# Hybrid decoder block on one core: the per-layer embedding's first loads in fewer DMAs on two queues, p's splits ahead of the weights', and the last row tile's last columns in two parts

## The chip, the core and the metric

One core of one Trainium2 chip runs the whole block in one launch. The metric is the device time of one execution, in microseconds (us). Beside it stands one profiled execution, in which the hardware profiler recorded each instruction; its times are what the views of the profile show.

The engines are TensorE (PE; its weight loads are a row of their own, PEld), VectorE (DVE), ScalarE (ACT), GpSimd (POOL), and SyncE (SP), which here issues the DMAs.

## The reference, cut to what matters

```python
h = x                                                     # (1024, 1024) f32
h = h + 0.5 * rms_norm(swiglu(rms_norm(h, g[0]), ffn1_gu, ffn1_down), g[1])
h = h + rms_norm(token_mixer(rms_norm(h, g[2]), ...), g[3])
h = h + 0.5 * rms_norm(swiglu(rms_norm(h, g[4]), ffn2_gu, ffn2_down), g[5])
gate = jax.nn.sigmoid(rms_norm(h, g[6]) @ w_ple_gate)     # (1024x1024) @ (1024x1024)
h = h + rms_norm(gate * (p @ w_ple), g[7])                # p (1024x256), w_ple (256x1024)
```

`rms_norm(y, g)` is `y * rsqrt(mean(y*y) + 1e-6) * g` over a row of 1024. The two lines at the end are the per-layer embedding: `p @ w_ple` depends on no other layer, and the gate needs the trunk's result.

## The kernel before, in words

The 1024 rows are worked in two halves of 512, and each half in four row tiles of 128. Every f32 operand of a matrix product is split into a high and a low part (`split`, L138 to L140): the high part is a cast to fp32r on ACT (L139), the low part is a subtraction on DVE (L140) that needs the high one. A product is then three matmuls (`PASSES`): high by high, high by low, low by high. `natural` (L213) issues these three for one row tile j, one k of 128 and up to 512 columns; `to_T` (L249) transposes blocks of 128 by 128 on TensorE (L253) into a PSUM bank of the pool `aux` and splits that.

The program runs five stages, one behind the other in the code: `embed` (the product of p and w_ple, put into a scratch array `e_d` in DRAM), the first FFN, the mixer, the second FFN, and `ple` (the gate's product, the norm and the result). The framework's scheduler decides in which order each engine's instructions are put; every engine takes its own list in order, and an instruction that waits holds up all that stand behind it on its engine. All DMAs of before are issued by SP, and a DMA that has to wait for its data or for a free buffer holds up the DMAs behind it.

`embed` (L1048): `load(0)` brings half 0 of p in four DMAs of 128 KB (L1055); `turn(0)` transposes the four tiles and splits them into the pair `pT`; `weight(0)` brings the 512 columns of w_ple for q = 0 in two DMAs of 256 KB (L1067) and splits them into `w`. Then three steps of the lane `la` follow: a lane is the generator `normed` (L329), which brings the rows of x (512 KB each, L1127), squares them (L342), scales them (L346, POOL's power L246, L348) and transposes and splits them into the operand `x0a` of the first FFN. Then come `weight(1)`, `load(1)`, and four sweeps, one for each half and q: 24 matmuls of 512 columns (L215) into four PSUM banks of the pool `mm`, whose content is copied to `e` (L1075 on ACT, L1077 on DVE) and written to `e_d` (256 KB each, L1078). Between the sweeps more steps of the lane are put, and after the second sweep `turn(1)`. `raw` is a pool of three tiles of 512 KB, shared by the weights of `embed` and those of the first FFN (`wcols`, L155, its load L158, `raw<-in_ffn_gu_dram` in the trace; its parts are named `hl`).

`ple` (L1101) holds the gate's weights in SBUF. For each half, row tile j and q it makes 24 matmuls of 512 columns and calls `take_gate` (L293): the load of `e` from `e_d` (L296), sigmoid on ACT (L299), the product on DVE (L300), square with the row's sum on ACT (L301), and the product with gamma on DVE (L302). After q = 1 `result` (L318) loads the residual row tile `res` from `h_d` (L320), adds the two sums and scales them on DVE (L308, L309), takes the power -1/2 on POOL (L246), and for each 512 columns adds to `res` (L324) and writes to `out` (L327). The last FFN's half 1 is finished in the shadow of `ple`'s half 0: the lane `finish` (L369) loads a row tile `h` (L374, 512 KB), adds the FFN's result in two halves (L314), writes it back to `h_d` (L379), squares it (L342), scales it (L348) and transposes it (L253) into the operand `xb` of `ple`'s half 1. `res` and these `h` tiles come from one pool, `n4`, of three buffers; `tick()` (L1118) is the point at which a step of the lane is put between the matmuls.

Of the kernel before, what the change touches and what calls it, by code (L numbers as in the profile page):

```python
# [9 lines left out]
F32 = mybir.dt.float32  # L10
F32R = mybir.dt.float32r
AF = mybir.ActivationFunctionType
ALU = mybir.AluOpType
# [3 lines left out]
P = 128  # L17
D = 1024
# [17 lines left out]
def hybrid_block(  # L36
# [39 lines left out]
    def nm(s):  # L76
        uid[0] += 1
        return f"{s}{uid[0]}"
# [40 lines left out]
    def mm_bank():  # L119
        return mm.tile([P, 512], F32, tag="mm", name=nm("mm"))  # L120
# [15 lines left out]
        return g  # L136

    def split(hi, lo, src):  # L138
        nc.scalar.copy(hi, src)  # L139
        nc.vector.tensor_tensor(lo, src, hi.bitcast(F32), op=ALU.subtract)  # L140

    def raw_tile():
        return wp.tile([P, 1024], F32, tag="raw", bufs=3, name=nm("raw"))
# [8 lines left out]
    def halves(t):  # L152
        return t.rearrange("p (q c) -> p q c", q=2)
# [59 lines left out]
    def natural(ps, ncol, sv, hl, j, first, last, resume=False):  # L213
        for n, (a, b) in enumerate(PASSES):
            nc.tensor.matmul(  # L215
                ps[:, :ncol],
                sv[b][:, j * P : (j + 1) * P],
                hl[:, a, :ncol],
                start=(first and n == 0),
                stop=(last and n == 2),  # L220
                skip_group_check=resume,
            )
# [21 lines left out]
    def power(var):  # L244
        r = sm.tile([P, 1], F32, tag="rstd", name=nm("rstd"))
        nc.gpsimd.tensor_tensor(r, var, mhalf[:, 0:1], op=ALU.pow)  # L246
        return r

    def to_T(src, nb, dst, j):  # L249

        ps = aux_bank()
        for b in range(nb):
            nc.tensor.transpose(ps[:, b * P : (b + 1) * P], src[:, b * P : (b + 1) * P], ident)  # L253
        v = ps[:, : nb * P].rearrange("p (b t) -> p b t", t=P)
        sl = (slice(None), slice(0, nb), slice(j * P, (j + 1) * P))
        split(dst[0][sl], dst[1][sl], v)
        return v

    def rows(half, j):
        t0 = half * HT + j * P  # L260
        return slice(t0, t0 + P)

    def cols(q):
        return slice(q * 512, (q + 1) * 512)

    class Post:
# [23 lines left out]
            nc.vector.tensor_tensor(t, t, self.g[:, cols(q)], op=ALU.mult)  # L290
            self.y[q, j] = t

        def take_gate(self, q, j, ps, e_src):  # L293

            e = yp.tile([P, 512], F32, tag="y", name=nm("e"))
            nc.sync.dma_start(e, e_src)  # L296
            y = yp.tile([P, 512], F32, tag="y", name=nm("y"))
            gate = n4.tile([P, 512], F32, tag="junk", bufs=2, name=nm("gate"))
            nc.scalar.activation(gate, ps, AF.Sigmoid)  # L299
            nc.vector.tensor_tensor(e, e, gate, op=ALU.mult)  # L300
            nc.scalar.activation(gate, e, AF.Square, accum_out=self.ss[j][:, q : q + 1])  # L301
            nc.vector.tensor_tensor(y, e, self.g[:, cols(q)], op=ALU.mult)  # L302
            self.y[q, j] = y

        def scale(self, j):
            s2 = self.ss[j]
# [8 lines left out]
                    res[:, cols(q)], self.y[q, j], r, res[:, cols(q)], op0=ALU.mult, op1=ALU.add  # L315
                )

        def result(self, j, res_src, dst):  # L318
            res = n4.tile([P, D], F32, tag="n4", name=nm("res"))
            nc.sync.dma_start(res, res_src)  # L320
            r = self.scale(j)
            for q in range(2):
                c = cols(q)
                nc.vector.scalar_tensor_tensor(  # L324
                    res[:, c], self.y[q, j], r, res[:, c], op0=ALU.mult, op1=ALU.add
                )
                nc.sync.dma_start(dst[:, c], res[:, c])  # L327
# [720 lines left out]
    def embed(pe, lane):  # L1048

        pT, pn = [], {}  # L1050

        def load(half):
            for j in range(4):
                pn[half, j] = pe.tile([P, 256], F32, tag="pn", bufs=8, name=nm("pn"))
                nc.sync.dma_start(pn[half, j], p[0, 0, rows(half, j), :])  # L1055

        def turn(half):
            pT.append([pe.tile([P, 2, HT], F32R, tag=f"pT{i}", name=nm("pT")) for i in range(2)])
            for j in range(4):
                to_T(pn[half, j], 2, pT[half], j)  # L1060

        def weight(q):

            raw = halves(raw_tile())
            hl = pe.tile([P, 2, 2, 512], F32R, tag="w", name=nm("w"))
            for k in range(2):
                nc.sync.dma_start(raw[:, k, :], w_ple[0, k * P : (k + 1) * P, cols(q)])  # L1067
            for k in range(2):
                split(hl[:, 0, k, :], hl[:, 1, k, :], raw[:, k, :])
            return hl  # L1070

        def keep(half, q, j, ps):
            e = pe.tile([P, 512], F32, tag="e", bufs=4, name=nm("e"))
            if j % 2 == 0:
                nc.scalar.copy(e, ps)  # L1075
            else:
                nc.vector.tensor_copy(e, ps)  # L1077
            nc.sync.dma_start(e_d[rows(half, j), cols(q)], e)  # L1078

        load(0)  # L1080
        turn(0)
        w = [weight(0)]
        for _ in range(3):
            next(lane)
        w.append(weight(1))
        load(1)
        for half in range(2):
            for q in range(2):
                ps = [mm_bank() for _ in range(4)]
                for k in range(2):  # L1090
                    sv = [t[:, k, :] for t in pT[half]]
                    for j in range(4):
                        natural(ps[j], 512, sv, w[q][:, :, k, :], j, k == 0, k == 1)
                for j in range(4):
                    keep(half, q, j, ps[j])
                for _ in range((1, 2, 1, 0)[2 * half + q]):
                    next(lane)
                if half == 0 and q == 1:
                    turn(1)

    def ple(xs, gi, res_d):  # L1101
        with tc.tile_pool(name="pl", bufs=5, reuse_waits="tile") as pl:
            g = gamma(gi)
            w = [load() for load in by_rows(w_ple_gate[0], 0, 512)[:3]]
            w += [load() for load in by_rows(w_ple_gate[0], 0, 512, pl)[3:]]
            w += [load() for load in by_rows(w_ple_gate[0], 512, 512, pl)]
            for half in range(2):
                xT, lane = xs[half]
                drain(lane)
                stat = parts(xT)  # L1110
                post = Post(g)
                for j in range(4):
                    for q in range(2):
                        ps = mm_bank()
                        for k in range(KD):
                            natural(ps, 512, stat(k), w[q * 4 + k // 2][:, :, k % 2, :], j, k == 0, k == KD - 1)
                        post.take_gate(q, j, ps, e_d[rows(half, j), cols(q)])
                        tick()  # L1118
                    post.result(j, res_d[rows(half, j), :], out[0, rows(half, j), :])


    xin = x[0]
# [55 lines left out]
```

## Time and profile before

| | us |
|---|---|
| time, median of 3 runs (lowest, highest) | 1850.26 (1848.3, 1851.3) |
| the profiled execution's own time | 1846.86 |
| its span, first to last record | 1845.1 |
| PE busy in the span | 1819.4 (99%) |
| DVE, ACT busy | 1262.5 (68%), 782.1 (42%) |
| granted TensorE clock, mean | 0.999 |

A row of the timeline gives the start in us, the duration in us, engine, line and operation, the tiles (out<-in), the shapes, and in brackets how long the engine sat idle before it and what ended that; "x4" behind a row means that four instructions of one kind are put together, and the duration is then that of the group. Matmuls are pipelined: of a group of n the last one's own 0.39 us is part of the duration. A row of the table of windows gives a stretch, then for each engine the busy time and the number of instructions that began in it, the granted clock, the mean busy share of the 16 DMA engines and the bytes moved in GB/s.

### The profile page before, as it was taken

What the parts mean: (1) busy time and instruction counts of PE and PEld (TensorE: products, weight loads), DVE (VectorE), ACT (ScalarE), POOL (GpSimd) and SP (SyncE); (2) the same over time, 40 slices, a digit from 0 to 9 for tenths busy, and PEclk for the clock granted to TensorE, in tenths of its full rate; (3) what the DMA queues carried; (4) which work ended last, traced back from release to release, by engine and by line L of the source; (5) the groups of instructions that cost most, each with busy time, mean ns of one, the idle gap of its engine ahead of it and who ended that gap; (6) DMA issues with size and microseconds to landing.
All of it is one profiled execution on the core that took longest, in us unless ns stands there. A gap on an engine that the chain in (4) does not pass through costs nothing.

```text
span 1845.1 us, 23321 instructions
## 1 busy us (share of the span) xinstructions
PE 1819.4 (99%) x8532; PEld 1511.0 (82%) x8532; DVE 1262.5 (68%) x1971; ACT 782.1 (42%) x1277; POOL 65.3 (4%) x96
## 2 busy tenths in 40 slices
PE   8999999999999999999999999999999999999998
PEld 6888888888888878888988887888888888888776
DVE  6598887776545678357535757978887865457773
ACT  5542222333434455457635545423233334444542
POOL 0000000000000100010000100000000000001010
PEclk9999999999999999999999999999999999999999
DMA  9766566566755766533433446655666667657563
GB/s 291 228 190 197 168 206 231 192 225 235 267 196 187 228 198 197 144 91 92 138 90 89 142 149 230 187 188 171 201 227 208 219 232 264 194 197 227 168 236 118
DMA packets 283522, 352.38 MB, mean 191 GB/s; under 512 B 19600, under 2 KB 164496, under 8 KB 283408
## 3 DMA queue, kind: packets, MB, share of 16 engines
q1 hardware_dynamic: 283408, 350.90, 59.2%
q8 instruction: 67, 1.10, 0.2%
q14 instruction: 47, 0.39, 0.1%
HBM read 249.65 MB, written 101.19 MB: 190 GB/s over the span
## 4 chain that ended last, share of the span: by engine, by line
PE 84%; DVE 9%; DMA 3%; issue 2%; ACT 1%; POOL 1%; SPq 0%; DVEq 0%; POOLq 0%; ACTq 0%
PE mm L167 42%; PE mm L215 28%; PE aux L215 10%; DMA raw<-in_ffn_gu_dram 1%; DVE hl L140 1%; PE aux L253 1%; DMA h<-in_x_dram 1%; DVE o L140 1%; DMA h_d<-h 1%; DVE h L314 1%; DVE h L348 1%; POOL rstd L246 1%; DVE s L140 1%; PE aux L925 0%; PE aux L849 0%
## 5 line engine op out<-in xcount | busy, mean ns | idle before, releaser
L167 PE MATMUL mm<-s,hl 128*128 128x512 f32 x1584 | 373.9, 389 | 0.5 <-ACT z L567 0.4
L167 PEld LDWEIGHTS mm<-s,hl 128*128 128x128 f32 x1584 | 297.1, 188 | 63.4 <-ACT z L567 1.3
L140 DVE TENSOR_TENSOR hl<-raw,hl 128x1024 fp32r<-128x1024 f32 (+1 forms) x124 | 143.1, 1155 | 164.2 <-ACT hl L139 164.0
L215 PE MATMUL mm<-o,o 128*128 128x512 f32 x1056 | 242.3, 390 | 1.9 <-DVE o L140 1.9
L215 PEld LDWEIGHTS mm<-o,o 128*128 128x128 f32 x1056 | 197.5, 188 | 43.7 <-DVE o L140 2.8
L140 DVE TENSOR_TENSOR o<-ra,o 128x1024 fp32r<-128x1024 f32 (+1 forms) x82 | 92.8, 1131 | 136.4 <-ACT o L139 136.4
L139 ACT CAST hl<-raw 128x1024 fp32r<-128x1024 f32 (+1 forms) x124 | 123.3, 996 | 141.7 <-PE mm L215 112.3
L215 PE MATMUL aux<-o,o 128*128 128x512 f32 x792 | 180.0, 389 | 0.0
L215 PEld LDWEIGHTS aux<-o,o 128*128 128x128 f32 x792 | 148.5, 188 | 31.2 <-DVE w L682 0.4
L139 ACT CAST o<-ra 128x1024 fp32r<-128x1024 f32 (+1 forms) x82 | 80.3, 980 | 209.7 <-PE aux L215 104.8
L167 PE MATMUL mm<-s,b 128*128 128x512 f32 x528 | 128.5, 392 | 0.9 <-DVE w L588 0.9
L167 PEld LDWEIGHTS mm<-s,b 128*128 128x128 f32 x528 | 98.2, 188 | 24.8 <-DVE w L588 4.0
L167 PE MATMUL mm<-xm_1h,hl 128*128 128x512 f32 x352 | 115.4, 389 | 0.0
L139 ACT CAST b<-raw 128x512 fp32r<-128x512 f32 x44 | 27.4, 623 | 191.9 <-PE mm L167 153.5
L140 DVE TENSOR_TENSOR o<-raw,o 128x1024 fp32r<-128x1024 f32 (+1 forms) x86 | 97.1, 1131 | 11.1 <-ACT o L139 11.1
L246 POOL TENSOR_TENSOR rstd<-var,mhalf 128x1 f32<-128x1 f32 x72 | 50.6, 711 | 1499.2 <-DVE var L309 1240.6
L139 ACT CAST o<-raw 128x1024 fp32r<-128x1024 f32 (+1 forms) x86 | 83.9, 978 | 7.1 <-issue 5.9
L215 PE MATMUL mm<-hl,xa_0h 128*128 128x512 f32 (+1 forms) x320 | 85.8, 350 | 0.9 <-ACT z L764 0.7
L215 PE MATMUL mm<-hl,xa_1h 128*128 128x512 f32 (+1 forms) x320 | 85.3, 349 | 0.0
L167 PEld LDWEIGHTS mm<-xm_1h,hl 128*128 128x128 f32 x352 | 66.1, 188 | 13.7
L139 ACT CAST hl<-tb 128x1024 fp32r<-128x1024 f32 x44 | 46.4, 1054 | 72.0 <-PE mm L167 69.6
L139 ACT CAST hl<-ta 128x1024 fp32r<-128x1024 f32 x44 | 46.4, 1055 | 64.6 <-PE mm L167 64.6
(276 smaller groups left out, 3312.6 us busy)
## 6 DMA issues: line engine op xcount, KB each, us to landing
raw<-in_ffn_gu_dram SPq DMA_DIRECT2D x112, 512.0 KB, 4.2
ra<-ha_d SPq DMA_DIRECT2D x68, 512.0 KB, 3.8
dr<-in_ffn_down_dram SPq DMA_DIRECT2D x44, 512.0 KB, 5.0
raw<-tb_d SPq DMA_DIRECT2D x40, 512.0 KB, 4.4
raw<-in_w_in_dram SPq DMA_DIRECT2D x40, 512.0 KB, 3.9
ha_d<-x SPq DMA_DIRECT2D x66, 256.0 KB, 2.2
raw<-in_ffn_down_dram SPq DMA_DIRECT2D x30, 512.0 KB, 4.4
h_d<-h SPq DMA_DIRECT2D x24, 512.0 KB, 3.9
```

The source lines that it names most:

```text
L139: nc.scalar.copy(hi, src)
L140: nc.vector.tensor_tensor(lo, src, hi.bitcast(F32), op=ALU.subtract)
L167: nc.tensor.matmul(ps, hl[:, a, k * P : (k + 1) * P], xo[b][:, k, :], start=(first and k == 0 and n == 0), stop=(last and k == 3 and n == ...
L215: nc.tensor.matmul(ps[:, :ncol], sv[b][:, j * P : (j + 1) * P], hl[:, a, :ncol], start=(first and n == 0), stop=(last and n == 2), skip_gr ...
L246: nc.gpsimd.tensor_tensor(r, var, mhalf[:, 0:1], op=ALU.pow)
L253: nc.tensor.transpose(ps[:, b * P : (b + 1) * P], src[:, b * P : (b + 1) * P], ident)
L314: nc.vector.scalar_tensor_tensor(res[:, cols(q)], self.y[q, j], r, res[:, cols(q)], op0=ALU.mult, op1=ALU.add)
L348: nc.vector.scalar_tensor_tensor(h[j], h[j], power(var), g, op0=ALU.mult, op1=ALU.mult)
```

## The change

In `embed`, half of p comes in one DMA of 512 KB (L1062 in the new code), and each half of w_ple in one DMA of 512 KB that ACT issues (`fetch`, L1074), both ahead of all else. The casts and subtractions of the weights are put behind those of `turn(0)` (`tc.issue_after`). In `ple`, the residual's load (L1131) and `e`'s load are issued ahead of the tile's matmuls, and the last row tile's last 512 columns are taken as two parts of 256: the sum of squares of the first 512 columns and that of the first part are put together ahead of the last square, with the norm's epsilon (L1143, L1144), so that one operation (L328) is left behind it.

```diff
@@ split, to_T
-        nc.scalar.copy(hi, src)
-        nc.vector.tensor_tensor(lo, src, hi.bitcast(F32), op=ALU.subtract)
+        return nc.scalar.copy(hi, src), nc.vector.tensor_tensor(lo, src, hi.bitcast(F32), op=ALU.subtract)
...
+        both = split(dst[0][sl], dst[1][sl], v)
+        return both if ends else v
@@ Post.take_gate
+        def load_e(self, e_src):
             e = yp.tile([P, 512], F32, tag="y", name=nm("e"))
             nc.sync.dma_start(e, e_src)
+            return e
...
+        def take_gate(self, q, j, ps, e, part=slice(0, 512), ss=None):
...
+            nc.scalar.activation(gate, e, AF.Square, accum_out=self.ss[j][:, q : q + 1] if ss is None else ss)
@@ Post.result
-        def result(self, j, res_src, dst):
-            res = n4.tile([P, D], F32, tag="n4", name=nm("res"))
-            nc.sync.dma_start(res, res_src)
-            r = self.scale(j)
+        def result(self, j, res, dst, ss=None):
+            if ss is None:
+                r = self.scale(j)
+            else:
+                var = sm.tile([P, 1], F32, tag="var", name=nm("var"))
+                nc.vector.tensor_scalar(var, ss[:, 1:2], ss[:, 0:1], 1.0 / D, op0=ALU.add, op1=ALU.mult)
+                r = power(var)
@@ embed
-            for j in range(4):
-                pn[half, j] = pe.tile([P, 256], F32, tag="pn", bufs=8, name=nm("pn"))
-                nc.sync.dma_start(pn[half, j], p[0, 0, rows(half, j), :])
+            pn[half] = pe.tile([P, 4, 256], F32, tag="pn", name=nm("pn"))
+            nc.sync.dma_start(
+                pn[half], p[0, 0, half * HT : (half + 1) * HT, :].rearrange("(j p) c -> p j c", p=P)
+            )
...
+        def fetch(q):
+            raw = halves(raw_tile())
+            nc.scalar.dma_start(raw, w_ple[0, :, cols(q)].rearrange("(k p) c -> p k c", p=P))
+            return raw
...
-            for k in range(2):
-                nc.sync.dma_start(raw[:, k, :], w_ple[0, k * P : (k + 1) * P, cols(q)])
...
+        raw = [fetch(q) for q in range(2)]
         load(0)
-        turn(0)
-        w = [weight(0)]
-        for _ in range(3):
-            next(lane)
-        w.append(weight(1))
+        with ExitStack() as behind:
+            for ins in turn(0):
+                behind.enter_context(tc.issue_after(ins.ins))
+            w = [weight(raw[0])]
+            for _ in range(3):
+                next(lane)
+            w.append(weight(raw[1]))
@@ ple
+                    last = half == 1 and j == 3
+                    res = n4.tile([P, D], F32, tag="n4", name=nm("res"))
+                    nc.sync.dma_start(res, res_d[rows(half, j), :])
+                    ss = sm.tile([P, 2], F32, tag="sse", name=nm("sse")) if last else None
                     for q in range(2):
...
+                        e = post.load_e(e_d[rows(half, j), cols(q)])
+                        for c0, n in ((0, 256), (256, 256)) if last and q == 1 else ((0, 512),):
+                            ps = mm_bank()
...
+                            post.take_gate(q, j, ps, e, slice(c0, c0 + n), ss[:, 1:2] if c0 else None)
+                            if last and q == 1 and not c0:
+                                s2 = post.ss[j]
+                                nc.vector.tensor_tensor(ss[:, 0:1], s2[:, 0:1], s2[:, 1:2], op=ALU.add)
+                                nc.vector.tensor_scalar(ss[:, 0:1], ss[:, 0:1], D * EPS, None, op0=ALU.add)
                         tick()
-                    post.result(j, res_d[rows(half, j), :], out[0, rows(half, j), :])
+                    post.result(j, res, out[0, rows(half, j), :], ss)
```

The scheduler puts more than these lines in a new order. In the rows that follow the number behind a name tells one tile from another.

The first place is ACT's list between the second and the third sweep of `embed`, where the casts of `x0a` and of half 1's `pT` stand. `hl_468` and `hl_473` are the first two weight tiles of the first FFN, whose loads are `raw_466` and `raw_471`. Before:

```order
L139 CAST hl_468<-raw_466 128x1024
L1075 COPY e_281<-mm_253 128x512
L1075 COPY e_287<-mm_255 128x512
L139 CAST x0a_0h<-aux_293 128x4x128
L139 CAST x0a_1h<-aux_300 128x4x128
L139 CAST x0a_0h<-aux_315 128x4x128
L139 CAST x0a_1h<-aux_322 128x4x128
L139 CAST pT_334<-aux_336 128x2x128
L139 CAST hl_473<-raw_471 128x1024
L139 CAST pT_334<-aux_341 128x2x128
```

Now, at the same place, with `raw_452`, `raw_457` and `raw_480` as the loads of the first three weight tiles of the FFN:

```order
L139 CAST x0a_1h<-aux_222 128x4x128
L350 ACTIVATE junk_516,ss_517<-h_478 128x1024
L1087 COPY e_267<-mm_239 128x512
L139 CAST hl_482<-raw_480 128x1024
L1087 COPY e_273<-mm_241 128x512
L139 CAST x0a_0h<-aux_279 128x4x128
L139 CAST x0a_1h<-aux_286 128x4x128
L139 CAST x0a_0h<-aux_301 128x4x128
L139 CAST x0a_1h<-aux_308 128x4x128
L139 CAST pT_320<-aux_322 128x2x128
L350 ACTIVATE junk_562,ss_563<-h_519 128x1024
L139 CAST pT_320<-aux_327 128x2x128
```

The first two weight casts of the FFN (`hl_454` and `hl_459`, loads `raw_452` and `raw_457`) now stand ahead of these rows, and the third one, `hl_482`, stands ahead of the second sweep's last copy, of the four casts of `x0a` and of all casts of half 1's `pT`. Before, the weight cast that stood among these was the second, and it stood behind the first cast of `pT`. The square of `h_519` (a row tile of x for half 1) is now between the first and the second cast of `pT`.

On SP the load `raw_480` now stands behind p twice, x five times (the four row tiles of half 0 and the first of half 1), gamma, the FFN's first two weight loads and the four writes of the first sweep to `e_d`; the two loads of w_ple are on ACT's queue. With these two it is the fifteenth half megabyte of the program.

The second place is SP's list in `ple`'s half 0, row tile 1, where the rows h2 and h3 of the last FFN's half 1 are loaded. Before (`h_14373` is h2, `h_14438` is h3, `res_14445` is the residual of row tile 1):

```order
L327 DMA out_dram<-res_14318 128x512 x2
L296 DMA e_14405<-e_d 128x512
L374 DMA h_14373<-h_d_94 128x1024
L374 DMA h_14438<-h_d_94 128x1024
L296 DMA e_14481<-e_d 128x512
L379 DMA h_d_95<-h_14373 128x1024
L320 DMA res_14445<-h_d_95 128x1024
L379 DMA h_d_95<-h_14438 128x1024
L296 DMA e_14539<-e_d 128x512
L327 DMA out_dram<-res_14445 128x512 x2
```

Now (`h_14361` is h2, `h_14426` is h3, `res_14315` is the residual of row tile 1):

```order
L1131 DMA res_14315<-h_d_95 128x1024
L382 DMA h_14361<-h_d_94 128x1024
L294 DMA e_14444<-e_d 128x512
L335 DMA out_dram<-res_14315 128x512 x2
L382 DMA h_14426<-h_d_94 128x1024
L387 DMA h_d_95<-h_14361 128x1024
L1131 DMA res_14442<-h_d_95 128x1024
```

The residual's load has moved ahead of h2's load, and the two writes of row tile 1's result stand between h2's load and h3's.

The third place is DVE's list at the same point. Before:

```order
L314 SCALAR_TENSOR_TENSOR h_14373<-z_13024,rstd_14378,h_14373 128x512
L314 SCALAR_TENSOR_TENSOR h_14373<-w_13028,rstd_14378,h_14373 128x512
L308 TENSOR_TENSOR var_14447<-ss_14229 128x1
L314 SCALAR_TENSOR_TENSOR h_14438<-z_13025,rstd_14443,h_14438 128x512
L309 TENSOR_SCALAR var_14447<-var_14447 128x1
L314 SCALAR_TENSOR_TENSOR h_14438<-w_13029,rstd_14443,h_14438 128x512
L346 TENSOR_SCALAR var_14503<-ss_14436 128x1
L300 TENSOR_TENSOR e_14481<-e_14481,gate_14484 128x512
L140 TENSOR_TENSOR xb_0l<-aux_14489,xb_0h 128x4x128
L302 TENSOR_TENSOR y_14483<-e_14481,g_14186 128x512
L140 TENSOR_TENSOR xb_1l<-aux_14496,xb_1h 128x4x128
L348 SCALAR_TENSOR_TENSOR h_14373<-h_14373,rstd_14505,g_12596 128x1024
```

Now:

```order
L332 SCALAR_TENSOR_TENSOR res_14315<-y_14344,rstd_14436,res_14315 128x512
L332 SCALAR_TENSOR_TENSOR res_14315<-y_14395,rstd_14436,res_14315 128x512
L318 SCALAR_TENSOR_TENSOR h_14361<-z_13010,rstd_14366,h_14361 128x512
L318 SCALAR_TENSOR_TENSOR h_14361<-w_13014,rstd_14366,h_14361 128x512
L139 TENSOR_TENSOR xb_0l<-aux_14477,xb_0h 128x4x128
L139 TENSOR_TENSOR xb_1l<-aux_14484,xb_1h 128x4x128
L354 TENSOR_SCALAR var_14491<-ss_14424 128x1
L305 TENSOR_TENSOR e_14444<-e_14444,gate_14472 128x512
L307 TENSOR_TENSOR y_14471<-e_14444,g_14172 128x512
L318 SCALAR_TENSOR_TENSOR h_14426<-z_13011,rstd_14431,h_14426 128x512
L318 SCALAR_TENSOR_TENSOR h_14426<-w_13015,rstd_14431,h_14426 128x512
L356 SCALAR_TENSOR_TENSOR h_14361<-h_14361,rstd_14493,g_12582 128x1024
```

The two additions that make row tile 1's result (`res_14315`) stand ahead of h2's two additions, where before they stood behind h2's scaling (L348). The scaling of h2 (L356 in the new code) stands behind both additions of h3, in both programs. On PE the transposes of h2 stand five matmuls later than before.

More of the change, by code (lines that the diff above doesn't have):

```diff
@@ L247, in power, with to_T @@
         return r
-    def to_T(src, nb, dst, j):
+    def to_T(src, nb, dst, j, ends=False):
         ps = aux_bank()
@@ L255, in to_T @@
         sl = (slice(None), slice(0, nb), slice(j * P, (j + 1) * P))
-        split(dst[0][sl], dst[1][sl], v)
-        return v
+        both = split(dst[0][sl], dst[1][sl], v)
+        return both if ends else v
     def rows(half, j):
@@ L291, in keep @@
             self.y[q, j] = t
-        def take_gate(self, q, j, ps, e_src):
+        def load_e(self, e_src):
             e = yp.tile([P, 512], F32, tag="y", name=nm("e"))
             nc.sync.dma_start(e, e_src)
-            y = yp.tile([P, 512], F32, tag="y", name=nm("y"))
-            gate = n4.tile([P, 512], F32, tag="junk", bufs=2, name=nm("gate"))
+            return e
+        def take_gate(self, q, j, ps, e, part=slice(0, 512), ss=None):
+            if (q, j) not in self.y:
+                self.y[q, j] = yp.tile([P, 512], F32, tag="y", name=nm("y"))
+            e, y = e[:, part], self.y[q, j][:, part]
+            ps = ps[:, : part.stop - part.start]
+            gate = n4.tile([P, 512], F32, tag="junk", bufs=2, name=nm("gate"))[:, part]
             nc.scalar.activation(gate, ps, AF.Sigmoid)
             nc.vector.tensor_tensor(e, e, gate, op=ALU.mult)
-            nc.scalar.activation(gate, e, AF.Square, accum_out=self.ss[j][:, q : q + 1])
-            nc.vector.tensor_tensor(y, e, self.g[:, cols(q)], op=ALU.mult)
-            self.y[q, j] = y
+            nc.scalar.activation(gate, e, AF.Square, accum_out=self.ss[j][:, q : q + 1] if ss is None else ss)
+            nc.vector.tensor_tensor(y, e, self.g[:, cols(q)][:, part], op=ALU.mult)
         def scale(self, j):
@@ L1059, in turn, with weight @@
             for j in range(4):
-                to_T(pn[half, j], 2, pT[half], j)
-        def weight(q):
+                last = to_T(pn[half][:, j, :], 2, pT[half], j, True)
+            return last
+        def fetch(q):
             raw = halves(raw_tile())
+            nc.scalar.dma_start(raw, w_ple[0, :, cols(q)].rearrange("(k p) c -> p k c", p=P))
+            return raw
+        def weight(raw):
             hl = pe.tile([P, 2, 2, 512], F32R, tag="w", name=nm("w"))
-            for k in range(2):
-                nc.sync.dma_start(raw[:, k, :], w_ple[0, k * P : (k + 1) * P, cols(q)])
             for k in range(2):
@@ L1112, in ple @@
                 for j in range(4):
+                    last = half == 1 and j == 3
+                    res = n4.tile([P, D], F32, tag="n4", name=nm("res"))
+                    nc.sync.dma_start(res, res_d[rows(half, j), :])
+                    ss = sm.tile([P, 2], F32, tag="sse", name=nm("sse")) if last else None
                     for q in range(2):
[L1114 to L1117, printed above, removed]
+                        e = post.load_e(e_d[rows(half, j), cols(q)])
+                        for c0, n in ((0, 256), (256, 256)) if last and q == 1 else ((0, 512),):
+                            ps = mm_bank()
+                            for k in range(KD):
+                                hl = w[q * 4 + k // 2][:, :, k % 2, c0 : c0 + n]
+                                natural(ps, n, stat(k), hl, j, k == 0, k == KD - 1)
+                            post.take_gate(q, j, ps, e, slice(c0, c0 + n), ss[:, 1:2] if c0 else None)
[3 more added lines that the diff above has]
+                                nc.vector.tensor_scalar(ss[:, 0:1], ss[:, 0:1], D * EPS, None, op0=ALU.add)
                         tick()
-                    post.result(j, res_d[rows(half, j), :], out[0, rows(half, j), :])
+                    post.result(j, res, out[0, rows(half, j), :], ss)
     xin = x[0]
```

## The prediction

> **What bounds the kernel now.** I read the page's busy times first, then the waits, then the timeline at both ends, and there only the stages that the change touches.
>
> ```profile
> span 1845.1 us, 23321 instructions
> PE 1819.4 (99%) x8532; PEld 1511.0 (82%) x8532; DVE 1262.5 (68%) x1971; ACT 782.1 (42%) x1277; POOL 65.3 (4%) x96
> ```
>
> TensorE is busy in all but 25.7 us. In the list of waits the largest of PE in the middle of the program is this one (total, times, longest):
>
> ```profile
> PE mm L167 <- DVE hl L140: 2.6, 3, 1.5
> ```
>
> So only the two ends have anything to give, and what is lost or gained there lasts to the end, unless it falls into one of these small waits of up to 1.5 us. The front, in the timeline (start, duration, engine, line, out<-in):
>
> ```profile
> 0.80 1.80 SPq L1055 DMA_DIRECT2D pn<-in_p_dram  x4
> ...
> 2.65 0.91 SPq L1067 DMA_DIRECT2D raw<-in_w_ple_dram  x2
> ...
> 3.00 2.05 PE L253 MATMUL aux<-ident,pn 128*128 128x128 f32 x8 [3.00 <-DMA pn<-in_p_dram]
> ...
> 7.04 1.29 ACT L139 CAST w<-raw 128x512 fp32r<-128x512 f32 x2 [4.96 <-DMA raw<-in_w_ple_dram]
> ...
> 10.03 1.17 ACT L139 CAST pT<-aux 128x256 fp32r<-128x256 f32 x4
> ...
> 10.43 7.86 PE L215 MATMUL mm<-w,pT 128*128 128x512 f32 x24 [5.38 <-ACT pT L139]
> ...
> 18.92 5.70 PE L215 MATMUL mm<-w,pT 128*128 128x512 f32 x24
> ...
> 20.47 0.77 SPq L158 DMA_DIRECT2D raw<-in_ffn_gu_dram  x1
> ...
> 21.64 1.05 ACT L139 CAST hl<-raw 128x1024 fp32r<-128x1024 f32 x1 [0.76 <-DMA raw<-in_ffn_gu_dram]
> ...
> 24.02 0.59 ACT L1075 COPY e<-mm 128x512 f32<-128x512 f32 x1 [0.78 <-PE mm L215]
> ...
> 25.09 0.59 ACT L139 CAST x0a_0h<-aux 128x512 fp32r<-128x512 f32 x1 [0.49 <-PE aux L253]
> ...
> 28.69 3.69 PE L215 MATMUL mm<-w,pT 128*128 128x512 f32 x15
> ```
>
> PE has p's transposes done at 5.05 and waits 5.38 for the casts of `pT`, which stand on ACT behind the weights' (7.04) and a square. From 10.43 it hardly stops. The table of windows shows the DMA engines full while that goes on (stretch; PE, PEld, DVE, ACT, POOL busy; clock; DMA share; GB/s):
>
> ```profile
> 0.00:3.00 3.00, 0.00 (x0) 0.03 (x1) 0.15 (x4) 1.28 (x1) 0.70 (x6) 1.00 0.30 94
> 3.00:10.50 7.50, 2.12 (x9) 1.26 (x9) 1.60 (x4) 2.76 (x6) 0.11 (x1) 1.00 0.98 314
> 10.50:15.50 5.00, 4.88 (x13) 3.39 (x14) 4.03 (x8) 4.03 (x9) 1.08 (x3) 1.00 1.05 392
> 18.00:30.00 12.00, 11.69 (x65) 9.20 (x64) 10.81 (x19) 8.64 (x17) 0.55 (x1) 1.00 0.97 300
> ```
>
> The tail behind the last matmul is a chain with nothing beside it:
>
> ```profile
> 1837.03 0.39 PE L215 MATMUL mm<-hl,xb_1h 128*128 128x512 f32 x1
> 1837.45 0.60 ACT L299 ACTIVATE gate<-mm 128x512 f32<-128x512 f32 x1 [3.36 <-PE mm L215]
> 1838.08 0.69 DVE L300 TENSOR_TENSOR e<-e,gate 128x512 f32<-128x512 f32 x1 [4.02 <-ACT gate L299]
> 1838.81 0.63 ACT L301 ACTIVATE gate<-e 128x512 f32<-128x512 f32 x1 [0.76 <-DVE e L300]
> ...
> 1839.56 0.16 DVE L308 TENSOR_TENSOR var<-ss 128x1 f32<-128x1 f32 x1
> 1839.76 0.15 DVE L309 TENSOR_SCALAR var<-var 128x1 f32<-128x1 f32 x1
> 1840.06 0.55 POOL L246 TENSOR_TENSOR rstd<-var,mhalf 128x1 f32<-128x1 f32 x1 [10.33 <-DVE var L309]
> 1840.64 1.42 DVE L324 SCALAR_TENSOR_TENSOR res<-y,rstd,res 128x512 f32<-128x512 f32 x2 [0.73 <-POOL rstd L246]
> 1841.42 1.00 SPq L327 DMA_DIRECT2D out_dram<-res  x2
> ```
>
> **The front: the first sweep.** The change puts p's four casts ahead of the weights' and sends w_ple through ACT's queue. ACT's two issues (0.45 each, from 0.91 for two of SP's) end with the table load (1.28) near 3.0, and ACT had nothing to do until 7.04: no cost, unless p came before 3.0. Fewer DMAs save SP some 1.3 of issuing (four of 1.80 become one of 0.45), but transposes can now begin only when all of p's half is there. p and both halves of w_ple, 0.52 MB each, now ask for the same 16 engines at once. By the windows 0.28 MB have moved by 3.0 and 314 GB/s follow: the first 1.05 MB are there at 3.0 + 0.77/0.314 = 5.5, all three (1.57 MB) at 7.1. With a cast of p's four tiles (1.17) and one of w's (0.65) behind them, the first matmul stands between 7.3 and 8.9, and at 11 if the x tiles on SP's queue share too, instead of 10.43: from -3.1 to +0.6.
>
> The Trainium skill's page "DMA: Bandwidth & Descriptors", section "Issuing engines are not separate DMA queues", says that DMAs started by different engines run on the same 16 DMA engines and interleave, so that a second issuer saves only the time to initiate. By that rule the early end of that range falls away; before had a single queue, so no trace here shows two.
>
> **The front: what the start is worth.** It is worth nothing if something later holds PE, and ACT's new order has that. The cast of the FFN's third weight tile (`hl_482`) stands ahead of the second sweep's last copy, the four casts of `x0a` and half 1's `pT`. With T for the landing of its load, ACT needs from T: that cast (1.05), the copy (0.59), and then what took from 25.09 to 28.69 before (3.60; a weight cast was in there, and a square of about its length is now). The third sweep then goes on at T + 5.24 instead of 28.69: it is late by T - 23.4.
>
> T by bytes: the load is the fifteenth half megabyte, 7.86 MB. With 2.64 MB moved by 10.5 (0.28 and 7.5 x 0.314), the rest takes 13.3 at 392 GB/s, so T = 23.8; at 314 it takes 16.6, T = 27.1; at 392 until 15.5 and 300 from there, as the windows have it, T = 26.4. By issue: before's second weight load, likewise behind the first sweep's four writes to `e_d`, was issued at 20.47, and one such load took
>
> ```profile
> raw<-in_ffn_gu_dram SPq DMA_DIRECT2D x1, 512.0 KB, 4.3
> ```
>
> from issue to landing, T = 24.8. I take 25.6, between the last two: **+2.2**, with +0.4 and +3.7 as ends. If the first sweep starts earlier, its writes are earlier too, but the bytes are not.
>
> **The row tiles h2 and h3 in ple.** The rows, with two of the list of DMAs (KB, us from issue to landing):
>
> ```profile
> 1769.44 0.80 SPq L374 DMA_DIRECT2D h<-h_d  x2
> ...
> 1772.91 0.68 DVE L302 TENSOR_TENSOR y<-e,g 128x512 f32<-128x512 f32 x1
> ...
> 1774.02 0.75 DVE L314 SCALAR_TENSOR_TENSOR h<-z,rstd,h 128x512 f32<-128x512 f32 x1 [0.43 <-DMA h<-h_d]
> ...
> 1779.55 1.27 DVE L348 SCALAR_TENSOR_TENSOR h<-h,rstd,g 128x1024 f32<-128x1024 f32 x1
> ...
> 1780.97 1.07 PE L253 MATMUL aux<-ident,h 128*128 128x128 f32 x8
> ```
>
> ```profile
> h<-h_d SPq DMA_DIRECT2D x1, 512.0 KB, 4.5
> ```
>
> ```profile
> res<-h_d SPq DMA_DIRECT2D x1, 512.0 KB, 5.0
> ```
>
> h2 and h3 were loaded together at 1769.44. Now the two writes of row tile 1's result stand on SP between them, and these wait for DVE. Its last product with gamma is done at 1773.6 (1772.91 + 0.68). From the first small operation behind it the tail shows 1.08 to the additions (1839.56 to 1840.64) and 1.78 more until both writes are issued (1841.42 + 1.00). So h3's load is issued at 1776.5 instead of 1769.9, and lands at 1781.0 (4.5) to 1781.5 (5.0). DVE makes h3's two additions (0.75 each) ahead of h2's scaling (1.27): h2 is done at 1781.0 + 1.5 + 1.3 = 1783.8, at the latest at 1784.3. PE comes to its transposes five matmuls later than before, 5 x 0.23 (18.92: 5.70 for 24) = 1.1, at 1782.1. It waits 1.7 to 2.2; **+2.0** taken, with 0 (scaling done by 1782.1 after all) and +3.0 (DVE's other work, 0.68 apiece, gets in between) as ends.
>
> **The tail.** The rows of 256 columns (tile pT; min, median, max ns) and two windows of PE alone, the first in narrow matmuls of 260 columns, the second in those of 512:
>
> ```profile
> L139 ACT CAST pT<-aux x8: 351/405/448, 10.0 to 28.7; 128x256 fp32r<-128x256 f32 x8
> L140 DVE TENSOR_TENSOR pT<-aux,pT x8: 415/416/425, 10.4 to 29.3; 128x256 fp32r<-128x256 f32 x8
> ```
>
> ```profile
> 731.00:736.00 5.00, 5.00 (x44) 1.00 0.38 83
> 1832.00:1837.00 5.00, 5.00 (x23) 1.00 0.32 111
> ```
>
> 24 matmuls become 48 narrow ones: 48 x 0.114 - 24 x 0.217 = +0.25. Behind the last: sigmoid 0.60 to 0.405 (-0.20), product 0.69 to 0.416 (-0.27), square likewise (-0.22), one small operation less (1839.56 to 1839.76, -0.20). The first part's own chain (about 1.9) has 24 x 0.114 = 2.7 of matmuls to hide in. The adding and writing of `res` stay. Sum **-0.65**, ends -0.4 and -1.0. The earlier loads of `e` and `res` wait for nothing that PE needs in half 1: nothing, covered by 5 us of matmuls in each part.
>
> **Sum.** +2.2 + 2.0 - 0.65 = +3.6 on 1846.86: 1850.5. The median of the runs shown lies 3.4 above the profiled execution; with that, **1853.9**. A difference under 0.2%, 3.7 us, is about what a measurement of this kernel can't tell from no change, and my sum lies at that bound.
>
> **Rivals.**
> *The rate after a wait (slower).* The 24 matmuls at 10.43, behind a wait of 5.38, took 7.86; the next 24, behind none, took 5.70. So a long wait may cost 2.2 more after it. It decides where the new wait at the third sweep is about as long as that one; mine is 2 to 4, and those of 1.5 in the middle are the only others the trace has. Then 1856.0. The Trainium skill's "TensorE: Matmul & The Clock Gate", Part 1, gives half clock after an idle window of about 3.4 us; by that rule only the top of my range for T would pay it, and the trace agrees for the wait of 5.38 and has none between that and 1.5.
> *One wait alone.* The load of h3 or the cast of `hl_482` comes in time, the other not: +3.6 less 2.2 or 2.0, 1851.7 to 1851.9. For it: T = 23.8 by the highest rate.
> *Neither.* PE is late nowhere: -0.65 and an unchanged front, 1849.6. The orders above speak against it.
> *The early start carries (faster).* The first matmul at 7.3 and nothing behind it holds PE: -3.1 - 0.65, 1846.5. It needs `hl_482`'s load by 20.3, 5.2 MB in 9.8 us from 10.5 on, 530 GB/s, far over the 392 of the windows, or waits of the FFN's start that would have come anyway. This is also where the change would do what its order says.
>
> **How the numbers follow.** Forecast 0.58 (its own range by the sums of the ends, +0.4 + 0 - 1.0 and +3.7 + 3.0 - 0.4: 1849.7 to 1856.6), of which 0.30 lie over 3.7 us. Rate after a wait 0.10, one wait alone 0.20 (0.01 slower), neither 0.05, early start 0.07. Slower 0.30 + 0.10 + 0.01 = 0.41; faster 0.07; the rest, 0.52, within 0.2%. The range holds all but the early start and the top: 1848.0 to 1857.5.
>
> **What would show it.** Right: PE waits about 2 before the third sweep of `mm<-w,pT` with ACT standing at a weight cast that waits for a DMA of in_ffn_gu, and about 2 before the transposes of h in ple behind DVE's L356, with h3's load issued near 1777 plus the front's shift; the tail 0.9 shorter from the last matmul to the end. Wrong: the third sweep begins before 28.7, h3's load issued together with h2's, or a first matmul near 7 with the same lead still there at 40.

## The result, and the profile after

The changed kernel takes 1872.78 us (median of 4 runs, 1871.48 to 1875.09); the kernel before, in the runs of the same comparison, 1849.28 (1846.77 to 1851.3). The ratio is 1.0123, with a 95% interval of 1.0111 to 1.0135: slower by 23 us, where 1853.9 was forecast and 1857.5 was the top of the range. The profiled execution took 1872.68. Of the experiments' runs below two lie far outside all others, one of ple_loads (7993.19) and one of front_behind (3733.52): the ratios leave them out, and without them the two medians are 1849.62 and 1847.28.

The page of the changed kernel, its first lines:

```profile
span 1871.0 us, 23365 instructions
...
PE 1844.1 (99%) x8556; PEld 1515.5 (81%) x8556; DVE 1265.5 (68%) x1974; ACT 782.6 (42%) x1280; POOL 66.2 (4%) x96
```

The span is 25.9 longer, and PE's busy time is 24.7 longer. PE is still busy in all but 26.9 us, against 25.7 before. So the time did not go into waits: PE needs longer for the same matmuls. The waits of PE that answer to those of before are small:

```profile
PE aux L252 <- DMA pn<-in_p_dram: 7.1, 1, 7.1
PE aux L252 <- DVE x0a_0l L139: 3.6, 1, 3.6
PE mm L166 <- DVE hl L139: 1.9, 3, 0.9
```

The groups of instructions say which matmuls are slower (line, engine, operation, out<-in, shape, count; then busy us, mean ns of one, idle before). Before:

```profile
L167 PE MATMUL mm<-s,hl 128*128 128x512 f32 x1584 | 373.9, 389 | 0.5 <-ACT z L567 0.4
L215 PE MATMUL mm<-o,o 128*128 128x512 f32 x1056 | 242.3, 390 | 1.9 <-DVE o L140 1.9
...
L215 PE MATMUL aux<-o,o 128*128 128x512 f32 x792 | 180.0, 389 | 0.0
...
L167 PE MATMUL mm<-xm_1h,hl 128*128 128x512 f32 x352 | 115.4, 389 | 0.0
```

After the change:

```profile
L166 PE MATMUL mm<-s,hl 128*128 128x512 f32 x1584 | 384.0, 395 | 0.5 <-ACT z L575 0.5
...
L214 PE MATMUL mm<-o,o 128*128 128x512 f32 x1056 | 248.3, 395 | 2.1 <-DVE z L609 1.2
...
L214 PE MATMUL aux<-o,o 128*128 128x512 f32 x792 | 184.5, 395 | 0.0
...
L166 PE MATMUL mm<-xm_1h,hl 128*128 128x512 f32 x352 | 115.7, 390 | 0.0
```

The first three groups, all of the two FFNs, have a mean of 395 ns instead of 389 or 390; the fourth, of the same shape and with the same weight tiles `hl`, stays at 390. From the start of one record to the start of the next it is 226.7 ns before and 232.9 after in `mm<-s,hl`, steadily and with a granted clock of 1.00. The diff touches none of these instructions, and their order is that of before.

The front, in the timeline after:

```profile
0.80 1.05 ACTq L1074 DMA_DIRECT2D raw<-in_w_ple_dram  x2
...
0.80 0.43 SPq L1062 DMA_DIRECT2D pn<-in_p_dram  x1
...
7.14 1.94 PE L252 MATMUL aux<-ident,pn 128*128 128x128 f32 x8 [7.14 <-DMA pn<-in_p_dram]
7.84 1.65 ACT L139 CAST pT<-aux 128x256 fp32r<-128x256 f32 x4 [4.68 <-PE aux L252]
...
10.06 7.14 PE L214 MATMUL mm<-w,pT 128*128 128x512 f32 x24 [0.98 <-ACT w L139]
...
18.76 0.43 SPq L157 DMA_DIRECT2D raw<-in_ffn_gu_dram  x1
...
26.16 1.04 ACT L139 CAST hl<-raw 128x1024 fp32r<-128x1024 f32 x1 [1.98 <-DMA raw<-in_ffn_gu_dram]
27.11 0.58 ACT L1087 COPY e<-mm 128x512 f32<-128x512 f32 x1
27.58 0.59 ACT L139 CAST x0a_0h<-aux 128x512 fp32r<-128x512 f32 x1
...
28.95 0.44 PE L252 MATMUL aux<-ident,pn 128*128 128x128 f32 x2 [3.64 <-DVE x0a_0l L139]
...
31.27 2.92 PE L214 MATMUL mm<-w,pT 128*128 128x512 f32 x7
```

p is there at 7.1, and the first sweep starts at 10.06 instead of 10.43. ACT then stands 1.98 at the cast of the FFN's third weight tile until its load is there at 26.16, and the third sweep goes on at 31.27 instead of 28.69. The windows of PE alone show the clock behind that wait:

```profile
30.00:32.00 2.00, 2.00 (x7) 0.53 0.84 211
32.00:34.00 2.00, 2.00 (x7) 0.62 0.83 279
```

The last matmul of the third and fourth sweep is 3.6 late (43.83 instead of 40.18): 2.6 from the wait, 1.1 from matmuls at half rate behind it.

In `ple` (SP, DVE, PE):

```profile
1800.83 0.45 SPq L382 DMA_DIRECT2D h<-h_d  x1
...
1804.97 0.75 DVE L318 SCALAR_TENSOR_TENSOR h<-z,rstd,h 128x512 f32<-128x512 f32 x1
...
1806.31 1.28 DVE L356 SCALAR_TENSOR_TENSOR h<-h,rstd,g 128x1024 f32<-128x1024 f32 x1
...
1807.74 1.07 PE L252 MATMUL aux<-ident,h 128*128 128x128 f32 x8 [0.91 <-DVE h L356]
```

PE is 24.5 late when it comes here, so h3's load is issued at 1776.3 on the scale of before, and over these transposes PE loses 1.1 more. The tail from the last matmul:

```profile
1863.82 0.28 PE L214 MATMUL mm<-hl,xb_1h 128*128 128x256 f32 x1
1864.14 0.38 ACT L304 ACTIVATE gate<-mm 128x256 f32<-128x256 f32 x1 [1.46 <-PE mm L214]
1864.55 0.43 DVE L305 TENSOR_TENSOR e<-e,gate 128x256 f32<-128x256 f32 x1 [1.50 <-ACT gate L304]
1865.01 0.42 ACT L306 ACTIVATE gate<-e 128x256 f32<-128x256 f32 x1 [0.49 <-DVE e L305]
...
1865.55 0.21 DVE L328 TENSOR_SCALAR var<-sse 128x1 f32<-128x1 f32 x1
```

From the last matmul's start to the span's end it is 7.2 (1871.0 - 1863.8) instead of 8.1.

What moved the middle stands in one line of the diff that I took for nothing: `ss = sm.tile([P, 2], F32, tag="sse", ...)`. A tile of 8 bytes in `sm`, a pool with four buffers, takes four times 32 bytes of each partition. All pools opened behind `sm` begin 128 bytes higher: the FFN's `s` from byte 162240 to 162368 of a partition, and with it the stationary operands `o` of the FFN's down part, the five tiles of the gate's weights in `pl` and others. The pools opened ahead of it stay, among them that of the weight tiles `hl` (94912). Matmuls with one operand ahead of `sm` and one behind it are the slow ones.

### The profile page after: what moved, and what is told of

Read it like the earlier page. It is cut to its first block, busy times and chain, and to the rows that moved or that the text cites. A ratio compares the mean times of both kernels' runs of the same rounds, so it can differ in the third digit from the quotient of the medians.

```text
span 1871.0 us, 23365 instructions
## 1 busy us (share of the span) xinstructions
PE 1844.1 (99%) x8556; PEld 1515.5 (81%) x8556; DVE 1265.5 (68%) x1974; ACT 782.6 (42%) x1280; POOL 66.2 (4%) x96
## 4 chain that ended last, share of the span: by engine, by line
PE 87%; DVE 6%; DMA 3%; issue 1%; ACT 1%; POOL 0%; SPq 0%; DVEq 0%; POOLq 0%; ACTq 0%
PE mm L166 45%; PE mm L214 28%; PE aux L214 10%; PE aux L252 1%; DMA raw<-in_ffn_gu_dram 1%; DVE hl L139 1%; DMA h<-h_d 1%; DVE h L318 1%; DVE h L356 1%; DVE o L139 1%; DVE s L139 0%; PE aux L933 0%; DMA ra<-ha_d 0%; POOL rstd L245 0%; PE aux L857 0%
## 5 line engine op out<-in xcount | busy, mean ns | idle before, releaser
L166 PE MATMUL mm<-s,hl 128*128 128x512 f32 x1584 | 384.0, 395 | 0.5 <-ACT z L575 0.5
L214 PE MATMUL mm<-o,o 128*128 128x512 f32 x1056 | 248.3, 395 | 2.1 <-DVE z L609 1.2
L214 PE MATMUL aux<-o,o 128*128 128x512 f32 x792 | 184.5, 395 | 0.0
```

Of the source, the lines that this page charges most:

```text
L166: nc.tensor.matmul(ps, hl[:, a, k * P : (k + 1) * P], xo[b][:, k, :], start=(first and k == 0 and n == 0), stop=(last and k == 3 and n == ...
L214: nc.tensor.matmul(ps[:, :ncol], sv[b][:, j * P : (j + 1) * P], hl[:, a, :ncol], start=(first and n == 0), stop=(last and n == 2), skip_gr ...
```

## The experiments

The theory (placement): a matmul of 512 columns takes some 6 ns longer when its two operands no longer lie alike, and the rest of the change does about what was forecast. The rival: the edits themselves, the second queue or the new order, slow the FFNs. Every kernel is compared with the kernel before on the same chip. Orders and instructions are unchanged wherever only the placement is edited.

**shift128**: the kernel before with the 128 bytes and nothing else.

```diff
@@ ple
+            sm.tile([P, 2], F32, tag="pad", bufs=4, name="pad")
             g = gamma(gi)
```

> The kernel before, with one unused tile of 4 x 32 bytes per partition in the pool sm and no other edit: every instruction and its order is that of before; all pools opened behind sm (the FFN's, the mixer's, embed's, ple's) lie 128 bytes higher, as they do in the changed kernel, where the new tile sse takes these 128 bytes. Placement theory (matmuls of 512 columns are slower where one operand has moved by 128 bytes against the other): the spacing of the FFNs' matmuls goes from 227 to 232 ns, some 4100 matmuls x 5.8 ns = 24 us, so 1849 goes to about 1872. Rival, the edits themselves (ACT's queue, the new order) slow the FFNs down: 1849, within 3.

1870.79 against 1849.98, ratio 1.0103 (1.0081 to 1.0125): unused bytes alone cost 20.8 us by the medians, 19 by the ratio (15 to 23). The group in its page has the changed kernel's mean:

```profile
L167 PE MATMUL mm<-s,hl 128*128 128x512 f32 x1584 | 383.6, 395 | 0.4 <-ACT z L567 0.3
```

**after_noshift**: the changed kernel with that tile elsewhere.

```diff
@@ ple
-                    ss = sm.tile([P, 2], F32, tag="sse", name=nm("sse")) if last else None
+                    ss = pl.tile([P, 2], F32, tag="sse", bufs=1, name=nm("sse")) if last else None
```

> The changed kernel with its tile sse taken from ple's own pool, behind the weights there, so that no other tile lies elsewhere than in the kernel before; the order of instructions is that of the changed kernel. Placement theory: the spacing is 227 everywhere again, and what is left is the front (+3.7 by the changed kernel's trace), ple's wait (+1.2) and the tail (-0.6): about 1853.5. Rival, the edits themselves: 1872.

1852.82 against 1849.98, ratio 1.0012 (1.0002 to 1.0023): 20 us of the 23.5 are gone with one line. The rival falls.

```profile
L166 PE MATMUL mm<-s,hl 128*128 128x512 f32 x1584 | 374.2, 389 | 0.5 <-ACT z L575 0.5
```

**all128**: does an operand's own address count, or the difference of the two?

```diff
@@ hybrid_block
     one = cst.tile([P, 1], F32, name="one")
+    cst.tile([P, 32], F32, name="pad")
```

> The kernel before with an unused tile of 128 bytes per partition ahead of all pools that hold operands: all operands of all matmuls move by 128 bytes together, none against another; the order is that of before. If the difference between a matmul's two operands counts (both 192 modulo 256 before, both 64 here): 1849. If an operand's own address counts (64 modulo 256 slow, 192 fast): all 7700 matmuls of 512 columns are slower by 5.8 ns or more, 45 us, about 1894.

1849.04 against 1849.98, ratio 0.9997 (0.9985 to 1.001). All operands lie 128 bytes higher, and nothing is slower:

```profile
L168 PE MATMUL mm<-s,hl 128*128 128x512 f32 x1584 | 374.2, 389 | 1.0 <-DVE hl L141 0.5
```

The difference counts.

**after_shift256**: the changed kernel with 128 bytes more in `sm` (the line of shift128), so that the pools behind it lie 256 higher.

> The changed kernel with another unused 128 bytes in the pool sm, so that the pools behind it lie 256 bytes higher than in the kernel before. If the offset modulo 256 counts: as without a shift, about 1853.5. If any shift against the kernel before counts, or the distance itself: 1872 or more.

1853.79 against 1849.98, ratio 1.0014 (1.0003 to 1.0024): as without a shift. The difference counts modulo 256.

**map1** and **map2**: several differences at once, by unused bytes ahead of the pools of single stages. In map1 (in words of 4 bytes; map2 has a=16, b=56, then a=48, b=8, then 16):

```diff
@@ gate_up (and so in down and ple, with pools of their own)
+            tc.tile_pool(name=f"pg_{label}", bufs=1, reuse_waits="tile") as pg,
             tc.tile_pool(name=f"fs_{label}", bufs=6, reuse_waits="tile") as so,
...
+            pg.tile([P, dict(a=8, b=24)[label]], F32, name="pad")
...
+            pd.tile([P, dict(a=16, b=40)[label]], F32, name="pad")
...
+            pp.tile([P, 48], F32, name="pad")
```

> The kernel before with unused bytes ahead of the pools of single stages, so that the two operands of a matmul lie apart by (modulo 256) 32 in the first FFN's gate and up part, 64 in its down part, 96 in the second FFN's gate and up part, 160 in its down part and 192 in ple; the mixer at 0. For the spacing of matmuls of 512 columns, if only half of 256 is bad: 227 ns in all these. If the spacing grows with the distance up to 128: 228, 229.5, 231, 231, 229.5. If any distance other than 0 is bad: 232 in all.

> The kernel before with other distances (modulo 256) between the two operands of a matmul: 64 in the first FFN's gate and up part, 192 in its down part, 224 in the second FFN's gate and up part, 32 in its down part, 64 in ple. If any difference other than 0 costs 5 to 7 ns a matmul, whichever operand is the moved one: 232 to 234 ns in all of these, about 1871. If the sign or the role counts: some of them at 227.

One run each: 1871.56 and 1867.29. The mean distance from one matmul's start to the next, of the records of 512 columns, gaps over 260 ns left out, by the address of the stationary operand less that of the moving one, modulo 256 (all runs together; a group names the moving operand first, as the rows do):

| difference | ns | groups |
|---|---|---|
| 0 | 226.6 to 229.5 | all of before and of all128, the mixer of all |
| 32 | 233.0 to 233.5 | `s,b`; `s,hl`; `o,o` |
| 64 | 232.3 to 233.4 | `o,o`; `hl,xb`; `s,b` |
| 96 | 232.9 | `s,b` |
| 128 | 231.8 to 233.0 | all groups of shift128 |
| 160 | 233.4 to 233.8 | `s,hl`; `o,o` |
| 192 | 228.6 to 230.2 | `s,hl`; `o,o`; `hl,xb` |
| 224 | 233.0 to 233.4 | `s,hl`; `s,b` |

"Any difference costs 5 to 7 ns" holds for all but 192 (64 the other way), which costs 2 to 3.5; there the expectation missed. Which operand was moved made no difference, the sign does. Only 0 is free. Groups of difference 0 inside the FFNs of the moved kernels are not in the table: where they stand directly behind a group of another difference, their first three to ten matmuls are still slow (at 142.57 us of the changed kernel 232, 232, 231, then 227), and their means lie between 226.8 and 230.5.

**front_only**: `embed`'s part of the change alone, on the kernel before (the functions split, to_T and embed of the diff).

> The kernel before with embed's part of the change alone (p in one DMA a half, w_ple through ACT's queue, p's splits first); no tile sse, so every tile lies where it lay before. By the traces of the changed kernel and of the one without the shift, PE is late by 3.7 to 4.8 at 40 us: 1849.5 goes to 1853.5 to 1854. By my prediction's term, +2.2: 1851.7. Rival, the lead at 40 us falls into PE's small waits further on: 1850.

1850.78 against 1849.56, ratio 1.0007 (0.9998 to 1.0016). In its profiled execution PE is 4.0 late at 40 us, and still 4.2 at the end; the median of 12 runs is only 1.2 above before's. The two don't contradict each other: before's profiled execution (1846.86), with which PE's times are compared here, is 2.7 below before's median, and front_only's (1851.06) 0.3 above its own. The 1853.5 to 1854 that I expected from the traces is missed, as it lies above the interval (1849.2 to 1852.5); my prediction's 1851.7 and the rival's 1850 lie within it.

**ple_loads**: the loads of `res` and `e` ahead of the tile's matmuls alone (`last = False` in ple's part of the change).

> The kernel before with the loads of res and e ahead of the tile's matmuls in ple, the last columns in one part as before, no shift. By the traces (PE later by 1.2 over the transposes of h2): +1.2, 1850.7. By my prediction's term, +2.0: 1851.5. Rival, nothing: 1849.5.

1849.66 against 1849.56, ratio 1.0 (0.9991 to 1.0009). In the trace PE loses 1.2 over h2's transposes, about as in the changed kernel (1.1); in the runs 1.2 can't be told from nothing.

**tail_only**: the last columns in two parts alone, loads where they were.

> The kernel before with the last row tile's last 512 columns taken in two parts, loads where they were, the sums' tile in ple's own pool so that nothing else moves. By my prediction's term -0.65: 1848.9, within the noise; in the trace the last matmul to the end is 0.9 shorter and the last 48 narrow matmuls take 0.2 longer than 24 wide ones. Rival, the second part of each row of weights costs more than it saves (PE up by over 0.9): 1850 or more.

1848.25 against 1849.56, ratio 0.9992 (0.9981 to 1.0003): on the side of the -0.65, not resolved.

**front_behind**: front_only, with the FFN's casts and squares on ACT behind half 1's casts of `pT` (`ends` are the last cast and subtraction of `turn(1)`).

```diff
+    behind = ExitStack()
+    for ins in ends:
+        behind.enter_context(tc.issue_after(ins.ins))
     x1 = ffn(ffn1_gu[0], ffn1_down[0], [(xa, la), (xb, lb)], hook1, 1, xin, h_d[0], "a")
+    behind.close()
```

> embed's part of the change alone, and the first FFN's casts and squares on ACT put behind half 1's casts of pT; no shift. If the cast of the third weight tile (hl_482) and the square before p's casts are what holds the third sweep up: PE is at 40 us where it was before or up to 0.8 earlier (embed's part alone: 4.0 later), no half rate from 30 on, and the time is 1849 or a little under. If the third sweep waits for the x tiles or p's half 1, which share the DMA engines: still 2 to 4 later, 1851 to 1853.

1847.67 against 1849.13, ratio 0.9986 (0.9977 to 0.9995). PE is 0.35 ahead of before at 40 us, and the third sweep goes on at 28.57, 22 matmuls in 5.29 and so at full rate:

```profile
28.57 5.29 PE L214 MATMUL mm<-w,pT 128*128 128x512 f32 x22
28.91 2.95 ACT L139 CAST hl<-raw 128x1024 fp32r<-128x1024 f32 x3
```

The three weight casts now stand behind `pT`, and the wait is gone although the same bytes share the DMA engines. So it was ACT's order that held PE, and not the DMA engines. This run moves the casts and the squares together; the one part seen by itself is the 1.98 that ACT stood at the third weight cast in the changed kernel.

**order_only**: p's splits in front, all loads on SP as before.

```diff
-        turn(0)
-        w = [weight(0)]
+        with ExitStack() as behind:
+            for ins in turn(0):
+                behind.enter_context(tc.issue_after(ins.ins))
+            w = [weight(0)]
```

> The kernel before with p's splits ahead of the weights' and nothing else: four DMAs for p and two for each half of w_ple on SP's queue as before. If the second queue is what makes p late (landed at 7.1 instead of 4.3): the first matmul at 7.8, 2.6 earlier than before, instead of 10.1. ACT has the cast of the second weight tile and the square of a row tile of x ahead of half 1's casts of pT, so the lead is partly lost at the third sweep: -2.6 to +1, 1847 to 1850.5. Rival, p lands late with any order: first matmul near 10.

1850.35 against 1849.13, ratio 1.001 (1.0 to 1.0021). The first sweep starts 3.4 earlier than before:

```profile
7.05 7.56 PE L214 MATMUL mm<-w,pT 128*128 128x512 f32 x24 [1.04 <-ACT w L139]
```

Two things differ from the changed kernel here: one queue, and p in four DMAs whose tiles are transposed as they land. That the second queue is a large part of it shows in what the queues (q1 is SP's, q10 ACT's) had moved by 5 us, in packets and MB; first the changed kernel, then order_only:

```profile
q10 hardware_dynamic: 190, 0.39, 24.8%
q1 hardware_dynamic: 342, 0.35, 24.3%
...
q1 hardware_dynamic: 691, 0.74, 57.1%
```

The same bytes move, but in the changed kernel over half of them are w_ple's, and p's 0.52 MB are not there. What the single DMA of p adds was not run by itself. But half 1 is held by the second weight tile's cast, for longer than expected: ACT stands 2.84 at it, this wait of PE is followed by half rate again, and PE is 4.1 late at 40 us where I expected it early.

```profile
25.50 1.04 ACT L139 CAST hl<-raw 128x1024 fp32r<-128x1024 f32 x1 [2.84 <-DMA raw<-in_ffn_gu_dram]
...
PE aux L252 <- DVE x0a_0l L139: 4.4, 1, 4.4
```

**best1**: order_only with the casts behind as in front_behind, and the tail of tail_only.

> p's splits first with the loads on SP's queue as before, the first FFN's casts and squares on ACT behind half 1's casts of pT, and the last columns in two parts, every tile at its old place. By the terms: -2.6 from the first matmul kept to the end, -0.65 at the tail: 1846.3 against 1849.5. If the small waits of the middle take up the lead: 1849.

1845.5 against 1849.13, ratio 0.9981 (0.9972 to 0.9989). PE is 2.0 ahead at 40 us. This version beats both kernels, by 0.2% the one before. Its page:

```profile
span 1843.4 us, 23379 instructions
...
PE 1819.7 (99%) x8556; PEld 1512.2 (82%) x8556; DVE 1263.2 (69%) x1974; ACT 782.9 (42%) x1280; POOL 66.3 (4%) x96
```

## Why the prediction was wrong

**The step that failed** is the sentence behind the second fence: "So only the two ends have anything to give". From PE's busy share I took the 1819 us of matmuls as given, and added up what happens between them. The change added nothing to the middle in the order of the instructions, but it moved the middle's operands in memory, and the duration of some 4100 matmuls is part of the sum. The missing term is 20 to 21 us by the medians: 20.8 when the shift is made alone, and 23.5 less 2.8 when it is taken out. By the spacings it is 1584 x 6.2 (`s,hl`) + 1800 x 5.8 (`o,o`) + 528 x 5.2 (`s,b`) + 216 x 5.3 ns (`hl,xb`), together 24.2 us, for the profiled executions; shift128's span is 25.7 longer than before's, 1870.8 against 1845.1, and the medians of the runs lie 20.8 apart. None of my rivals had it, and the part on what would make the prediction wrong named no such thing. A new tile in the pool `sm` stood in the diff; I costed its operations and not its place.

**Without that term** the forecast is not contradicted: +3.6 was summed, 1853.9 given, and after_noshift is 1852.82, which is +2.8, or +0.4 to +4.3 by its interval. The times do not confirm the terms one by one: alone, the three parts came to +1.2 (front_only), +0.1 (ple_loads) and -1.3 (tail_only), 0.0 together, with intervals over 3 us wide each. What follows on the terms is read from the traces.

- *First sweep*: 7.3 to 11 was given, 10.06 measured. p's half landed at 7.1, at the time at which I had all three loads there, and from there it took 2.9 to the first matmul where I had 1.8: the four casts wait for the transposes one by one (1.65 instead of 1.17, begun 0.7 behind the first transpose). With one queue and p in four DMAs (order_only) the first sweep starts at 7.05. The Trainium skill's "DMA: Bandwidth & Descriptors", section "Issuing engines are not separate DMA queues", has DMAs of different issuers share the 16 engines; the trace agrees (0.35 MB through SP's queue and 0.39 through ACT's by 5 us), and here the sharing delays the load that was needed first; with the single DMA of p it comes to 3.0 at the first matmul.
- *Third sweep*: T = 25.6 was taken, 26.16 measured; late by 2.6 against +2.2. The mechanism (ACT's order, with the cast of the third weight tile ahead of `pT`) is shown by front_behind, for the casts and squares together. That T came out so near was luck in part: its load was issued at 18.76, not 20.5, and took 7.4 to land, not 4.3.
- *The rate after a wait*: the rival with a chance of 0.10 came true in small. Behind a wait of 3.6 the windows show a clock of 0.53 and 0.62 and PE loses 1.1 more, not 2.2: only four matmuls in a row start 427 ns apart or nearly so. The 2.2 was misread: I took before's slow first sweep (7.86) as the price of the wait of 5.38, but the first sweep is as slow behind waits of 1: 7.14 in the changed kernel behind 0.98, and 7.56 in order_only behind 1.04. It belongs to the program's start in all three: its first six or more matmuls start 426 ns or more apart.
- *h2 and h3*: the load was issued at 1776.3 on before's scale against 1776.5, but landed 4.1 later instead of 4.5 to 5.0; PE lost 1.1 (1.2 in after_noshift and ple_loads) against +2.0. The mechanism was right, its size too large. By itself it is below what the runs tell.
- *Tail*: 0.9 shorter behind the last matmul, as summed.

The rival *the early start carries* was rightly thought little of for this order; best1 shows that it carries when ACT's casts and squares do not stand in its way: of 3.4 at the first sweep 2.0 are left at 40 us.

## What to carry to other kernels

Before costing an edit's instructions, look at what it allocates: one small tile in a pool opened early moves every pool behind it, and where PE is the bound, 6 ns on each of 4100 matmuls outweighed all the waits that I had summed. After a change, compare the mean duration of the largest groups of unchanged instructions before hunting for waits. And an earlier start is worth what the next in-order engine lets through: put casts for later stages behind those that the present stage waits for.

## What the runs showed of the hardware

A matmul of 512 columns with fp32r operands follows the one before after 226.7 ns (229.5 in the slowest group) when the addresses of stationary and moving operand agree modulo 256, and after 232 to 234 when they differ, except for a difference of 192 (228.6 to 230.2); the common offset makes no difference (226.8 at 64 and 226.7 at 192 in `s,hl`). Why is open: the records of the weight loads do not get longer (188 ns in `s,hl` of before and of shift128), but no run here separates the weight load, which overlaps the matmul before, from the matmul's own reading, and no difference finer than 32 bytes was tried.

In after_noshift PE fell to half rate behind a wait of 2.8 us (windows of PE alone in the second fence), matmuls starting 427 ns apart for about 4 us; the waits of 1.5 in the middle of before never did that.

```profile
29.20 1.29 PE L252 MATMUL aux<-ident,pn 128*128 128x128 f32 x4 [2.78 <-DVE x0a_0l L139]
```

```profile
32.00:34.00 2.00, 2.00 (x6) 0.50 0.87 295
34.00:36.00 2.00, 2.00 (x7) 0.57 0.52 163
```

Near 2.2 us it goes either way: in order_only a wait of 2.19 was followed by half rate (so was one of 2.31 in tail_only), in all128 one of 2.17 was not. The wait and the window behind it (PE alone), order_only first:

```profile
1762.08 0.80 PE L214 MATMUL mm<-hl,xb_1h 128*128 128x512 f32 x1 [2.19 <-ACT hl L139]
1762.00:1764.00 2.00, 1.92 (x5) 0.50 1.01 384
...
1758.77 0.50 PE L216 MATMUL mm<-hl,xb_1h 128*128 128x512 f32 x1 [2.17 <-ACT hl L140]
1758.00:1760.00 2.00, 1.23 (x5) 1.00 1.03 419
```

The Trainium skill's "TensorE: Matmul & The Clock Gate", Part 1, names an idle window of about 3.4 us for it; here waits of 2.2 to 2.8 were enough in three runs.
